# Ten closing steps split by token half: five weight blocks kept instead of reloaded, more entry products, and weight casts two blocks ahead

## The chip, the cores and the metric

The program runs on one core of a Trainium2 chip. The metric is the device time of one execution in microseconds. Five engines work side by side, each through its own queue of instructions in order: TensorE (PE, matmuls; PEld are its weight loads), VectorE (DVE), ScalarE (ACT), GpSimd (POOL) and SyncE (SP, which here issues all DMAs). They wait for each other by semaphores.

## The reference, cut to what matters

One decoder layer over 256 tokens of width 2048 in float32. A vector `mod`, made from the condition `c`, gives nine groups of shift, scale and gate; each is 2048 wide.

```python
cond = silu(c)
mod = cond @ ada_w + ada_b                  # 9 x 2048: sh1 sc1 gt1 sh2 sc2 gt2 sh3 sc3 gt3
h = rmsnorm(x, norm_g[0]) * (1 + sc1) + sh1
x = x + 0.5 * gt1 * ((silu(h @ wg) * (h @ wu)) @ wd)      # FFN 1, d_ff 5632
h = rmsnorm(x, norm_g[1]) * (1 + sc2) + sh2
x = x + gt2 * mixer(h)                      # 8 forgetting-attention heads, 8 gated-delta heads, w_in, w_out
h = rmsnorm(x, norm_g[2]) * (1 + sc3) + sh3
x = x + 0.5 * gt3 * ((silu(h @ wg) * (h @ wu)) @ wd)      # FFN 2
return rmsnorm(x, final_norm)
```

Each stage needs the normalised x of the stage before, so a token's last sum, its squares, its root and its scaling stand between two stages.

## The kernel before, in words

**Weights.** All large weights come as a stream of blocks: 128 x 1024 float32 (512 KB, eight tiles of 128 x 128), in the order in which they are used. `Stream.block` (L98) issues a block's DMA on SP into a tile `wraw` and casts it on ACT to `whi` (L106, a shorter float format). `Stream.low` (L109) subtracts on DVE: `wlo` = raw - `whi` (L113). Activations are split in the same way into a high and a low part (`hs`, `hid`, `oh`). There are three places each for `wraw`, `whi` and `wlo`, and in the FFNs and at the mixer's end a fourth (`W.more`), taken by each block whose number leaves 3 when divided by 4. `Stream.next` (L126) hands out the next tiles; at each new block it also adds a pace (`RATE`, by block number) to a sum, and whenever this reaches 1 it fetches one more column of the condition's matrix (`ada_col`; DMA `adat`, 1 MB, and a reduction on DVE, L286, three blocks later), unless `W.quiet` is set. With `W.early` (the mixer's projections) a block's load, cast and subtraction are written in the program one block ahead of its use (`ahead`).

**Products.** `products` (L572) multiplies a step (four tiles, 512 output columns) by the two halves of the tokens: for each half three matmuls, high x high (L576), low x high (L577), high x low (L579). In the mixer's projections by rows the three are L857, L858, L859; by columns, L517 and L518.

**Stages.** `ffn` runs `gate_up` and `down` for two parts of d_ff each; `mixer` runs projections, the heads' chains (a planner with due times puts pieces of them between the projections' tiles) and the output product `po`. A stage's last 512 output columns are made in `last_block` (L665). Its last ten steps (`S_OUT`) are first done for half 0 alone, then for half 1 alone, so that half 0's sum, squares, root and scaling can run while PE works on half 1. The weights of the last four of these steps are held in the usual places; those of the first six (`S_AGAIN`, `twice`) are fetched a second time as three further blocks, cast and subtracted again, for half 1. There are three such ends: FFN 1, mixer, FFN 2. Then one block of the next stage is loaded ahead, its cast tied behind half 0's root (`roots[0]`), its subtraction behind half 0's factor (`yins[0]`).

**Entries.** `modulate` (L425) first makes sure that all columns of the next stage's shift and scale are there (`ada_need`), builds the gains, and makes a list of work: `half(0)` and `half(1)` (rows of `hs` 0 and 1 for one token half: scale x to `xn`, transpose on PE into `pxt`, then ACT and DVE write the high and low parts, L448 to L453), then pairs of rows for both halves. It is called two steps before the end, with `half(0)`. The next stage does its first `S_IN` = 2 row groups for half 0 alone (four products in the mixer, six in FFN 2), then the same for half 1, then the rest for both. `residual` (L534) is the sum at a stage's end: gate multiply (`rs`, L540), add (L541), square (L384), and in the last columns `norm_rstd` (L396 to L401).

The framework orders each engine's queue by a simulated schedule in which program order sets the priority; `tc.issue_after` ties an instruction behind another of the same engine.

Of the kernel before, what the change touches and what calls it, by code (L numbers as in the profile page):

```python
# [16 lines left out]
P = 128  # L17
# [12 lines left out]
S_OUT, S_AGAIN, S_IN = 10, 6, 2  # L30
# [7 lines left out]
N_TILES = 5392 + 3 * 4 * S_AGAIN  # L38
# [4 lines left out]
RATE = ((0, 0.5), (24, 0.34), (56, 0.45), (68, 0.35), (112, 0.45), (168, 0.38), (266, 0.4), (282, 0.0), (300, 0.17), (412, 0.125))  # L43
# [33 lines left out]
class Stream:  # L77


    def __init__(self, nc, w, raw, hi, lo):  # L80
# [9 lines left out]
        self.pairs, self.early, self.ready = set(), set(), {}  # L90
# [6 lines left out]

    def block(self, b, cast_after=None):  # L98

        at = PAIR if b in self.pairs else 0  # L100
        raw, hi, lo = self.more if self.more and b % 4 == 3 else (self.raw, self.hi, self.lo)
        r = raw.tile([P, WB * P], F32, name="wraw")
        self.last = self.nc.sync.dma_start(r, self.w[b]).ins
        self.h = hi.tile([P, WB * P + 64], F32R, name="whi")[:, at : at + WB * P]
        with nullcontext() if cast_after is None else self.tc.issue_after(cast_after):
            self.cast = self.nc.scalar.copy(self.h, r).ins  # L106
        return r, lo, at

    def low(self, r, lo, at):  # L109

        self.l = lo.tile([P, WB * P + 64], F32R, name="wlo")[:, at : at + WB * P]
# [14 lines left out]
    def next(self, mat, k, n, width=1):  # L126
        i = len(self.order)
        if i % WB == 0:
# [8 lines left out]
            if b + 1 in self.early:  # L137
                self.ahead(b + 1)
# [13 lines left out]
def layer_kernel(ctx: ExitStack, tc: tile.TileContext, xrow, c, adaw, cols, cst, fng, w, out, order, dbg=None):  # L152
# [272 lines left out]
    def modulate(which, m_sh, m_sc):  # L425
# [3 lines left out]

        def turn(ps, j, t):  # L430

            xn = tmp.tile([P, T], F32, name="xn", bufs=4)
            if t:
                V.tensor_scalar(xn, X(t, j * P, T), ystd[t], None, ALU.mult)
            else:
                A.activation(xn, X(t, j * P, T), AF.Copy, scale=ystd[t])
# [18 lines left out]
        def half(t):  # L455

            ps = psf("pxt")
            turn(ps, 0, t)
            for j in range(2):
                scale(ps, j, t * P, P)  # L460
# [14 lines left out]
    hq = {"todo": []}  # L475

    def h_need(k, t=1):

        while hq["todo"] and (hq["todo"][0][0] < k + AHEAD if hq["todo"][0][0] > 1 and t else hq["todo"][0][:2] <= (1, t)):
            hq["todo"].pop(0)[2]()  # L480
# [106 lines left out]
    def gate_up(which, f0, f1, hp, sp, chunks, lead, need):  # L587
# [55 lines left out]
        for ci, (k0, k1) in enumerate(chunks):  # L643
            for gi in range(0, len(cgs), 2):
# [6 lines left out]
                first = S_IN if need is h_need and pb else 0  # L651
                wts = {(k, e): one(pb[e], *e, k, k0, k1, (0,)) for k in range(k0, k0 + first) for e in pb}
                for (k, e), wt in wts.items():
                    one(pb[e], *e, k, k0, k1, (1,), wt)
                for k in range(k0 + first, ks):
                    for e in pb:
                        one(pb[e], *e, k, k0, k1)
# [7 lines left out]
    def last_block(steps, weights, one, ps, m_gt, squares, begin):  # L665

        twice, held = steps[-S_OUT : S_AGAIN - S_OUT], steps[S_AGAIN - S_OUT :]
        for f in steps[:-S_OUT]:
            one(f, weights(f), (0, 1), False)
        for f in twice:  # L670
            one(f, weights(f), (0,), False)
        held = [(f, weights(f)) for f in held]
        for f, wt in held:
            one(f, wt, (0,), f == steps[-1])
# [5 lines left out]
        for i in range(1, n):  # L680
            W.ahead(b + i)
        for f, wt in held:
            one(f, wt, (1,), False)
        if squares != "final":
            W.held = [yins[0]]
            W.ahead(b + n, roots[0])
        for f in twice:
            if f == twice[-2] and begin:
                modulate(*begin)
                hq["todo"].pop(0)[2]()  # L690
# [792 lines left out]
```

## Time and profile before

| what | us |
|---|---|
| median of 3 runs | 2037.12 |
| lowest, highest | 2032.08, 2038.51 |
| profiled execution | 2035.86 |
| its span, first to last instruction | 2034.1 |
| mean granted TensorE clock | 0.991 |

In the views, a busy row gives start or span, the engine, the source line, the operation and the tiles out<-in; square brackets hold the idle time of the engine just before and what ended it. A windows row gives the length of the window, the busy time of PE, PEld, DVE, ACT and POOL (with the number of instructions), the granted TensorE clock, the share of time in which DMA engines were busy, and GB/s.

### The profile page before, as it was taken

The numbers are of one execution on the slowest core, as the hardware profiler recorded it, in microseconds if no ns is written. First come the engines' busy times: TensorE is split into PE (matmuls) and PEld (weight loads), VectorE is DVE, ScalarE is ACT, GpSimd is POOL, SyncE is SP. The second block draws the span as 40 slices with busy tenths as digits, with TensorE's granted clock in tenths as the row PEclk, the third lists the DMA queues.
The fourth block names the chain that finished last, engine by engine and source line by source line (L and its number), as shares of the span: only waits on it lengthen the run. The fifth ranks groups of instructions, "written<-read, shape, count | busy, mean of one in ns | idle before, by whom it ended". The sixth has DMA issues, their size and how long they took to land.

```text
span 2034.1 us, 25528 instructions
## 1 busy us (share of the span) xinstructions
PE 1987.4 (98%) x9385; PEld 1648.0 (81%) x9385; DVE 1494.7 (73%) x2096; ACT 1001.4 (49%) x1451; POOL 2.6 (0%) x15
## 2 busy tenths in 40 slices
PE   8999999999999999998999999999999999999998
PEld 5788888888888887887888888788888888888886
DVE  6899999898787886689877887765566565455455
ACT  5544444343433456685657655644444333444444
POOL 0000000000000000000000000000000000000000
PEclk8999999999999999999999999999999999999999
DMA  8989898999788886564656577666666665555554
GB/s 323 349 326 349 314 344 333 354 387 375 298 331 338 325 304 243 185 214 155 209 205 220 187 259 267 219 218 239 249 243 231 239 238 196 187 192 189 207 195 167
DMA packets 134511, 528.92 MB, mean 260 GB/s; under 512 B 18489, under 2 KB 23785, under 8 KB 116081
## 3 DMA queue, kind: packets, MB, share of 16 engines
q1 hardware_dynamic: 134386, 527.29, 71.2%
q8 instruction: 73, 1.20, 0.2%
q14 instruction: 52, 0.43, 0.1%
HBM read 521.82 MB, written 5.41 MB: 259 GB/s over the span
## 4 chain that ended last, share of the span: by engine, by line
PE 91%; DVE 3%; DMA 3%; ACT 2%; issue 1%; ACTq 0%; DVEq 0%; SPq 0%
PE pgu L579 15%; PE pgu L577 15%; PE pgu L576 15%; PE pd L577 8%; PE pd L576 8%; PE pd L579 8%; PE pp L517 6%; PE pp L518 3%; DMA wraw<-in_w_dram 2%; DVE wlo L113 2%; PE pv L857 1%; PE pv L859 1%; PE pv L858 1%; PE po L577 1%; PE po L576 1%; PE po L579 1%
## 5 line engine op out<-in xcount | busy, mean ns | idle before, releaser
L106 ACT CAST whi<-wraw 128x1024 fp32r<-128x1024 f32 x683 | 714.8, 1051 | 833.7 <-PE pgu L577 280.3
L113 DVE TENSOR_TENSOR wlo<-wraw,whi 128x1024 fp32r<-128x1024 f32 x683 | 826.3, 1222 | 385.9 <-ACT whi L106 382.8
L576 PE MATMUL pgu<-whi,hs 128*128 128x512 f32 x1408 | 552.1, 394 | 14.8 <-ACT hs L411 6.5
L577 PE MATMUL pgu<-whi,hs 128*128 128x512 f32 x1408 | 550.5, 392 | 0.3
L579 PE MATMUL pgu<-wlo,hs 128*128 128x512 f32 x1408 | 438.0, 391 | 1.2 <-DVE wlo L113 1.2
L286 DVE CUSTOM_DVE_ANT_0 adat<-adat,cs,colt 128x2048 f32<-128x2048 f32 x140 | 328.7, 2348 | 41.4 <-DMA adat<-in_ada_dram 40.6
L576 PEld LDWEIGHTS pgu<-whi,hs 128*128 128x128 f32 x1408 | 266.0, 189 | 73.4 <-ACT hs L411 7.4
L579 PEld LDWEIGHTS pgu<-wlo,hs 128*128 128x128 f32 x1408 | 265.1, 189 | 58.4 <-DVE wlo L113 3.2
L577 PEld LDWEIGHTS pgu<-whi,hs 128*128 128x128 f32 x1408 | 266.2, 189 | 56.6 <-DVE hs L453 1.1
L576 PE MATMUL pd<-whi,hid 128*128 128x512 f32 x704 | 274.7, 390 | 0.0
L577 PE MATMUL pd<-whi,hid 128*128 128x512 f32 x704 | 273.9, 389 | 0.0
L517 PE MATMUL pp<-hs,whi 128*128 128x512 f32 x656 | 242.3, 405 | 8.7 <-ACT whi L106 8.7
L579 PE MATMUL pd<-wlo,hid 128*128 128x512 f32 x704 | 220.0, 389 | 0.0
L518 PE MATMUL pp<-hs,wlo 128*128 128x256 f32 x656 | 189.7, 290 | 1.3 <-DVE wlo L113 1.3
L576 PEld LDWEIGHTS pd<-whi,hid 128*128 128x128 f32 x704 | 132.2, 188 | 27.7 <-issue 0.2
L579 PEld LDWEIGHTS pd<-wlo,hid 128*128 128x128 f32 x704 | 132.2, 188 | 27.5
L577 PEld LDWEIGHTS pd<-whi,hid 128*128 128x128 f32 x704 | 132.2, 188 | 27.1
L517 PEld LDWEIGHTS pp<-hs,whi 128*128 128x128 f32 x656 | 124.8, 190 | 32.1 <-ACT whi L106 9.9
L518 PEld LDWEIGHTS pp<-hs,wlo 128*128 128x128 f32 x656 | 125.5, 191 | 2.5 <-DVE wlo L113 1.9
L857 PE MATMUL pv<-whi,hs 128*128 128x512 f32 x128 | 52.3, 411 | 0.5 <-ACT whi L106 0.3
L859 PE MATMUL pv<-wlo,hs 128*128 128x512 f32 x128 | 50.8, 398 | 0.0
L858 PE MATMUL pv<-whi,hs 128*128 128x512 f32 x128 | 50.6, 395 | 0.0
(313 smaller groups left out, 1369.9 us busy)
## 6 DMA issues: line engine op xcount, KB each, us to landing
wraw<-in_w_dram SPq DMA_DIRECT2D x683, 512.0 KB, 4.4
adat<-in_ada_dram SPq DMA_DIRECT2D x140, 1024.0 KB, 7.6
gtr<-gd SPq DMA_DIRECT2D x12, 256.0 KB, 6.2
rw<-rowd SPq DMA_DIRECT2D x24, 128.0 KB, 3.8
adaf<-in_ada_dram SPq DMA_DIRECT2D x4, 512.0 KB, 10.0
x<-in_xr_dram SPq DMA_DIRECT2D x4, 512.0 KB
adaf<-in_ada_dram SPq DMA_DIRECT2D x2, 1024.0 KB
xd<-x SPq DMA_DIRECT2D x4, 512.0 KB
```

Of the source, the lines that this page charges most:

```text
L106: self.cast = self.nc.scalar.copy(self.h, r).ins
L113: self.sub = self.nc.vector.tensor_tensor(self.l, r, self.h.bitcast(F32), ALU.subtract).ins
L286: V.tensor_tensor_reduce(t, t, cs, HALF.get(m, 1.0), L("adab", q, 1), ALU.mult, ALU.add, mod[:, q : q + 1])
L517: PE.matmul(ps, wt[0], act.rearrange("p a t -> p (a t)"), start=first, stop=False)
L518: PE.matmul(ps[:, :T], wt[1], act[:, 0], start=False, stop=last)
L576: PE.matmul(ps[t], hi_(t), wh, start=first, stop=False)
L577: PE.matmul(ps[t], lo_(t), wh, start=False, stop=False)
L579: PE.matmul(ps[t], hi_(t), wl, start=False, stop=last)
L857: PE.matmul(pv[m][t], hs[:, k, 0, sl], wh, start=(k == 0), stop=False)
L858: PE.matmul(pv[m][t], hs[:, k, 1, sl], wh, start=False, stop=False)
L859: PE.matmul(pv[m][t], hs[:, k, 0, sl], wl, start=False, stop=(k == KD - 1))
```

## The change

What it does:

- The last ten steps' five blocks are all kept until half 1. The first three go, high and low part together, into one tile each of a pool that has room inside the stage (`home`: the FFN's `hid` pool; in the mixer a new pool `holdp` of three, opened after the heads' pools are closed). The last two stay in the usual places. Half 1 takes these two first, then the three. No block is loaded a second time: the stream has 5392 tiles (674 blocks) instead of 5464 (683).
- While half 1 runs, three blocks of the next stage are loaded, cast and subtracted: one before half 0's sum, one after two steps, its cast behind `roots[0]`, one after four.
- `modulate` makes the work list finer (`n_ahead` = 2: rows 0 to 3 in pieces of one half); two pieces of half 0 are done at the end. Half 1's first `xn` is written directly behind its root, and the next block's subtraction is tied behind it.
- At entries eight products of half 0 (FFN 2) or six (mixer) come before half 1's, four blocks or three.
- In the mixer's projections a block's load is written three blocks ahead and its cast and subtraction two ahead. The pace of adaLN columns is 0.25 from block 338 on (0.17 before), and it is silenced from the middle of the mixer's third output block on.

The diff, cut to its core:

```diff
-S_OUT, S_AGAIN, S_IN = 10, 6, 2
+S_OUT, S_HOME = 10, 6
-RATE = ((0, 0.5), (24, 0.34), (56, 0.45), (68, 0.35), (112, 0.45), (168, 0.38), (266, 0.4), (282, 0.0), (300, 0.17), (412, 0.125))
+RATE = ((0, 0.5), (24, 0.34), (56, 0.45), (68, 0.35), (112, 0.45), (168, 0.38), (266, 0.4), (282, 0.0), (300, 0.17), (338, 0.25), (412, 0.125))
...
+    def load(self, b):
+
+        more = self.more and self.home is None and b % 4 == self.odd
+        r = (self.more[0] if more else self.raw).tile([P, WB * P], F32, name="wraw")
+        self.last = self.nc.sync.dma_start(r, self.w[b]).ins
+        return r, more
...
+        r, more = self.loaded.pop(b) if b in self.loaded else self.load(b)
+        hi, lo = self.more[1:] if more else (self.hi, self.lo)
+        if self.home:
+            both = self.home()
+            self.h, lo = both[:, : WB * P], both[:, WB * P :]
+        else:
+            self.h = hi.tile([P, WB * P + 64], F32R, name="whi")[:, at : at + WB * P]
+        if cast_after is None and self.cast_held:
+            cast_after = self.cast_held.pop(0)
...
-            if b + 1 in self.early:
-                self.ahead(b + 1)
+            if b + 3 in self.early:
+                self.loaded[b + 3] = self.load(b + 3)
+            for a in (b + 1, b + 2):
+                if a in self.early and a not in self.ready:
+                    self.ahead(a)
...
-        hq["todo"] = [(1, 0, lambda: half(0)), (1, 1, lambda: half(1))]
-        hq["todo"] += [(j + 1, 1, lambda j=j: pair(j)) for j in range(2, KD, 2)]
+        js = range(0, 2 * n_ahead, 2)
+        hq["todo"] = [((j, t), lambda j=j, t=t: half(j, t)) for t in range(2) for j in js]
+        hq["todo"] += [((j, None), lambda j=j: pair(j)) for j in range(2 * n_ahead, KD, 2)]
+        hq["normed"] = normed
...
-                first = S_IN if need is h_need and pb else 0
+                ahead = [(k, e) for k in range(k0, ks) for e in pb]
+                n = 8 if hq["todo"] else 0
...
+        W.home = home
+        held = []
+        for f in steps[-S_OUT:]:
+            if len(held) == S_HOME:
+                W.home = None
+            held.append((f, weights(f)))
+            one(f, held[-1][1], (0,), f == steps[-1])
+        held = held[S_HOME:] + held[:S_HOME]
         assert len(W.order) % WB == 0 and not W.ready
         b = len(W.order) // WB
-        n = S_AGAIN * 4 // WB
-        W.ahead(b)
+        if begin:
+            W.more, W.odd = None, (b + 3) % 4
+            W.ahead(b)
         residual(ps[0], 0, 3, m_gt, squares)
+        W.held = [yins[0]]
+        for n, (f, wt) in enumerate(held):
+            if begin and n == 2:
+                W.ahead(b + 1, roots[0])
+            if begin and n == 4:
+                W.ahead(b + 2)
+            if begin and n == S_OUT - 2:
+                modulate(*begin)
+                for _ in range(begin[-1]):
+                    h_pop()
+            one(f, wt, (1,), n == S_OUT - 1)
         residual(ps[1], 1, 3, m_gt, squares, yins[0])
+        if begin:
+            W.held = [sums[1], hq["normed"](0, 1)]
+            W.cast_held = [None, roots[1]]
...
+            n = 6 if hq["todo"] else 0
             held = []
+            for m, k in todo[:n]:
+                held.append((m, k, W.next(m, k, 4 * grp, 4)))
+                some(m, k, (0,), held[-1][2])
+            for i, (m, k, wt) in enumerate(held):
                 some(m, k, (1,), wt)
+                if i == 1:
+                    W.ahead(len(W.order) // WB)
+            if n:
+                W.early = set(range(len(W.order) // WB + 1, W.last_early))
...
+                if (b, i) == (2, KD // 2):
+                    W.quiet = True
...
+                holdp = mx.enter_context(tc.tile_pool(name="holdp", bufs=S_HOME // 2))
```

More of the change, by code (lines that the diff above doesn't have):

```diff
@@ L89, in __init__ @@
         self.sub = None
-        self.pairs, self.early, self.ready = set(), set(), {}
+        self.pairs, self.early, self.ready, self.loaded = set(), set(), {}, {}
+        self.home, self.odd, self.cast_held = None, 3, []
     def behind(self, later=True):
@@ L428, in modulate, with normed @@
         W.quiet = True
-        def turn(ps, j, t):
[L432 to L436, printed above, removed]
+        made = {}
+        def normed(j, t):
+            xn = made[j, t] = tmp.tile([P, T], F32, name="xn", bufs=4)
+            if t:
+                return V.tensor_scalar(xn, X(t, j * P, T), ystd[t], None, ALU.mult).ins
+            return A.activation(xn, X(t, j * P, T), AF.Copy, scale=ystd[t]).ins
+        def turn(ps, j, t):
+            if (j, t) not in made:
+                normed(j, t)
+            xn = made.pop((j, t))
             for q in range(2):
@@ L453, in scale, with half @@
             V.tensor_tensor(hs[:, j, 1, tok], t, hs[:, j, 0, tok].bitcast(F32), ALU.subtract)
-        def half(t):
+        def half(j, t):
             ps = psf("pxt")
-            turn(ps, 0, t)
-            for j in range(2):
-                scale(ps, j, t * P, P)
+            turn(ps, j, t)
+            for q in range(2):
+                scale(ps, j + q, t * P, P)
         def pair(j):
@@ L663, in gate_up, with last_block, down @@
         return hid
-    def last_block(steps, weights, one, ps, m_gt, squares, begin):
-        twice, held = steps[-S_OUT : S_AGAIN - S_OUT], steps[S_AGAIN - S_OUT :]
+    def last_block(steps, weights, one, ps, m_gt, squares, begin, home):
         for f in steps[:-S_OUT]:
             one(f, weights(f), (0, 1), False)
[L670 to L674, printed above, removed]
+        W.home = home
[6 more added lines that the diff above has]
+        held = held[S_HOME:] + held[:S_HOME]
         assert len(W.order) % WB == 0 and not W.ready
         b = len(W.order) // WB
-        n = S_AGAIN * 4 // WB
-        W.ahead(b)
+        if begin:
+            W.more, W.odd = None, (b + 3) % 4
+            W.ahead(b)
         residual(ps[0], 0, 3, m_gt, squares)
[L680 to L688, printed above, removed]
+        W.held = [yins[0]]
[5 more added lines that the diff above has]
+            if begin and n == S_OUT - 2:
                 modulate(*begin)
-                hq["todo"].pop(0)[2]()
-            one(f, weights(f), (1,), f == twice[-1])
+                for _ in range(begin[-1]):
+                    h_pop()
+            one(f, wt, (1,), n == S_OUT - 1)
         residual(ps[1], 1, 3, m_gt, squares, yins[0])
-        if squares != "final":
-            W.held = [sums[1], yins[1]]
-    def down(which, f0, f1, hid, m_gt, squares, begin=None):
+        if begin:
+            W.held = [sums[1], hq["normed"](0, 1)]
+            W.cast_held = [None, roots[1]]
+    def down(which, f0, f1, hid, m_gt, squares, hp, begin=None):
         fs = list(range(f0, f1))
@@ L705, in down @@
             if ends:
-                last_block(fs, lambda f: W.next(("d", which), f, 4 * b, 4), one, ps, m_gt, squares, begin)
+                home = lambda: hp.tile([P, 2 * WB * P], F32R, name="hold", tag="hid")
+                last_block(fs, lambda f: W.next(("d", which), f, 4 * b, 4), one, ps, m_gt, squares, begin, home)
             else:
@@ L732, in ffn @@
                     fng_load()
-                down(which, f_[half], f_[half + 1], hid, m_gt, *((squares, begin) if half else (None,)))
+                down(which, f_[half], f_[half + 1], hid, m_gt, *((squares, hp, begin) if half else (None, hp)))
             W.more = None
@@ L1329, in mixer @@
             if b == 3:
-                last_block(list(range(KD)), weights, one, ps, 5, "mid", (2, 6, 7))
+                last_block(list(range(KD)), weights, one, ps, 5, "mid", (2, 6, 7, 2),
+                           lambda: holdp.tile([P, 2 * WB * P], F32R, name="hold"))
                 break
```

42 lines of the change are left out of this document (18 added, 24 removed).

## The prediction

> **What bounds the kernel now.** I read the page's head first, then the grouped waits of the matmul engine, then the windows view in 20 us slices, and only then the timelines of the slices that are not full.
>
> ```profile
> PE 1987.4 (98%) x9385; PEld 1648.0 (81%) x9385; DVE 1494.7 (73%) x2096; ACT 1001.4 (49%) x1451; POOL 2.6 (0%) x15
> L106 ACT CAST whi<-wraw 128x1024 fp32r<-128x1024 f32 x683 | 714.8, 1051 | 833.7 <-PE pgu L577 280.3
> L113 DVE TENSOR_TENSOR wlo<-wraw,whi 128x1024 fp32r<-128x1024 f32 x683 | 826.3, 1222 | 385.9 <-ACT whi L106 382.8
> PE pp L517 <- ACT whi L106: 8.7, 4, 2.9
> 759.17 0.39 PE L576 MATMUL pd<-whi,hid 128*128 128x512 f32 x1
> 759.40 0.39 PE L577 MATMUL pd<-whi,hid 128*128 128x512 f32 x1
> 759.62 0.39 PE L579 MATMUL pd<-wlo,hid 128*128 128x512 f32 x1
> ```
>
> PE is busy 98%: matmuls start every 0.227 us, and the change neither adds nor removes one. So it can win only where PE stands still or runs at a lower clock. A product of one token half is three matmuls, 0.68 us; a block of weights is two steps, 1.36 us for one half and 2.72 us for both.
>
> The places, by the windows view (length, then PE, PEld, DVE, ACT, POOL busy, granted clock, DMA share, GB/s):
>
> ```profile
> 774.00:778.00 4.00, 1.62 (x7) 0.69 (x6) 2.94 (x9) 2.79 (x6) 0.00 (x0) 1.00 0.92 330
> 778.00:784.00 6.00, 5.86 (x21) 4.23 (x22) 3.76 (x10) 3.29 (x10) 1.30 (x5) 0.72 0.92 325
> 880.00:900.00 20.00, 16.74 (x94) 14.39 (x93) 17.95 (x63) 19.09 (x56) 0.12 (x1) 0.91 0.73 221
> 920.00:940.00 20.00, 18.02 (x107) 16.09 (x108) 17.87 (x47) 9.91 (x22) 0.55 (x3) 0.91 0.64 202
> 880.00:960.00 80.00, 70.95 (x425) 61.98 (x423) 73.53 (x248) 58.56 (x144) 0.66 (x4) 0.96 0.57 185
> 1060.00:1220.00 160.00, 157.13 (x941) 135.74 (x940) 129.97 (x320) 102.47 (x221) 0.00 (x0) 1.00 0.63 220
> 1284.00:1288.00 4.00, 0.22 (x1) 0.00 (x0) 4.00 (x6) 1.98 (x3) 0.00 (x0) 0.99 0.41 133
> 1288.00:1296.00 8.00, 7.66 (x21) 5.59 (x22) 5.45 (x13) 2.41 (x8) 0.00 (x0) 0.58 0.49 166
> ```
>
> First entry (first FFN to mixer, 772 us): 4 - 1.62 = 2.38 us idle, 0.14 more, and 6 x 0.28 = 1.68 us at the lower clock: 4.2 us. Second entry (mixer to second FFN, 1284 us): 3.78 + 0.34 idle and 8 x 0.42 = 3.36 us of clock: 7.5 us. The mixer at 880 to 960 us: 80 - 70.95 = 9.05 us idle and, in two slices, 2 x 20 x 0.09 = 3.6 us of clock. The first 130 us and the chain behind PE's last product are touched by no edit.
>
> **Part 1, the last ten steps.** Nine blocks (three at each of three ends) are no longer loaded twice: nine casts of 1.05 us, nine subtractions of 1.22 us, nine transfers of 512 KB. All lie beside a full PE, so they are worth nothing by themselves; what they leave is room. In the mixer's end a reload's cast stood at the head of ACT, waiting for PE to free a place, with half 0's square behind it:
>
> ```profile
> 1278.33 1.05 ACT L106 CAST whi<-wraw 128x1024 fp32r<-128x1024 f32 x1 [3.02 <-PE po L577]
> 1279.29 0.62 ACT L384 ACTIVATE jq<-x 128x512 bf16<-128x512 f32 x1
> 763.39 3.54 SPq L826 DMA_DIRECT2D xd<-x  x3
> ```
>
> With five blocks kept (three in inner places that need no release, two in the usual three), the third usual place takes the next stage's first block, and the second and third follow as half 1 frees places: all three are cast and subtracted before the stage begins, where before only one was. Also, at 763.39 three copies of x sat 3.5 us at the head of SP's queue until half 0's x was there; they are tied behind the last weight load issued, which is now the third block's, so these loads no longer wait behind them.
>
> **Part 2, more products at entries.** Half 1's chain (gate, sum, square, root, normalise, transpose, scale) sets when its products can start. At the first entry:
>
> ```profile
> 771.86 0.69 DVE L540 TENSOR_TENSOR rs<-pd,gtr 128x512 f32<-128x512 f32 x1 [0.16 <-PE pd L579]
> 773.39 0.62 ACT L384 ACTIVATE jq<-x 128x512 bf16<-128x512 f32 x1
> 774.53 1.05 ACT L106 CAST whi<-wraw 128x1024 fp32r<-128x1024 f32 x1 [0.41 <-DMA wraw<-in_w_dram]
> 775.48 0.29 ACT L396 ACTIVATE nstd<-ss 128x1 f32<-128x1 f32 x1
> 776.26 0.16 DVE L401 SCALAR_TENSOR_TENSOR nstd<-nya,nstd 128x1 f32<-128x1 f32 x1
> 777.47 0.61 DVE L434 TENSOR_SCALAR xn<-x,nstd 128x256 f32<-128x256 f32 x2
> 777.87 0.88 PE L439 MATMUL pxt<-colt,xn 128*128 128x128 f32 x6 [2.33 <-DVE xn L434]
> 778.35 0.46 ACT L451 ACTIVATE hs<-pxt,mod,g 128x128 fp32r<-128x128 f32 x1 [0.32 <-PE pxt L439]
> ```
>
> The reader sees a cast of 1.05 us (late because its transfer was late) between square and root, and 1.2 us between the factor (776.42) and xn (777.47) in which DVE subtracted a block. Without these two, and with x right behind rs, the chain is rs 0.69, x 0.69, square and its read 0.75, root 0.3, four small DVE operations 0.6 to 0.7, xn 0.35: 3.4 us from the end of half 1. The change issues xn first by name and has the three blocks ready. Half 0 then has six products (4.1 us) instead of four (2.7 us) to cover it. What stays open is transposes, scale and their hand-over if they stand behind the six products: from 777.87 to the end of 778.35 + 0.46 is 0.94 us. I take 1.1 us left of 4.2: **3.1 us** gained; bounds 0.5 (the chain as late as now, only two products more) and 4.2.
>
> At the second entry two adaLN reductions stand in DVE before half 1's chain:
>
> ```profile
> 1283.82 0.40 PE L579 MATMUL po<-wlo,oh 128*128 128x512 f32 x1
> 1281.15 2.35 DVE L286 CUSTOM_DVE_ANT_0 adat<-adat,cs,colt 128x2048 f32<-128x2048 f32 x1
> 1284.56 2.35 DVE L286 CUSTOM_DVE_ANT_0 adat<-adat,cs,colt 128x2048 f32<-128x2048 f32 x1
> 1286.83 0.69 DVE L540 TENSOR_TENSOR rs<-po,gtr 128x512 f32<-128x512 f32 x1
> 1287.43 0.17 DVE L422 SCALAR_TENSOR_TENSOR g<-mod,colt 128x16 f32<-128x16 f32 x1
> 1287.69 0.46 ACT L451 ACTIVATE hs<-pxt,mod,g 128x128 fp32r<-128x128 f32 x1 [1.82 <-DVE g L422]
> L275 SPq DMA_DIRECT2D adat<-in_ada_dram x21: 328/425/1977, 809.9 to 1274.3; - x21
> ```
>
> PE's last product ended at 1284.2, rs came 2.6 us later, and even half 0's rows waited for the gains. In the new pace the mixer must fetch the same 21 columns. Counted by blocks, now three lower: five blocks at 0.40 (2.0), 38 at 0.17 (6.5), then 0.25 from block 338; the remaining 12.5 take 50 blocks, to 388, and the pace is silenced at 398. So both reductions leave the entry. The 5.5 us of eight half-0 products then cover a chain of 3.4 us plus scaling. Two things are late next: the hand-over again (0.9), and the fourth block, which eight products need after six (4.1 us). Its place opens only when the old tiles over it are free, in my estimate at half 1's last product. The windows show such a transfer: issued at 1284.7, gone by 1287.5.
>
> ```profile
> L103 SPq DMA_DIRECT2D wraw<-in_w_dram x4: 327/328/328, 1284.7 to 1293.5; - x4
> 1285.50:1287.50 2.00, 0.00 (x0) 0.00 (x0) 2.00 (x4) 0.38 (x1) 0.00 (x0) 1.00 0.81 262
> ```
>
> 2.8 us and a cast of 1.05 make 3.9 to 4.1 us: just in time, or some tenths late. I take 1.3 us left of 7.5: **6.2 us** gained; bounds 3.0 and 7.5.
>
> The waits that are added: the fourth block's subtraction behind half 1's sum, the fifth's cast behind its root and its subtraction behind xn. PE needs none of them before about 4 us after half 1, and the chain goes ahead of them. Two more transposes in the end phase are moved, not added.
>
> **Part 3, mixer blocks cast two ahead, loaded three ahead.** The waits on casts, in the order of time:
>
> ```profile
> 940.00:960.00 20.00, 17.04 (x113) 14.83 (x111) 19.07 (x72) 14.55 (x38) 0.00 (x0) 1.00 0.24 86
> 893.86 0.50 PE L517 MATMUL pp<-hs,whi 128*128 128x512 f32 x1 [2.57 <-ACT whi L106]
> 921.98 0.50 PE L517 MATMUL pp<-hs,whi 128*128 128x512 f32 x1 [2.82 <-ACT whi L106]
> 958.22 0.51 PE L517 MATMUL pp<-hs,whi 128*128 128x512 f32 x1 [2.88 <-ACT whi L106]
> ACT whi L106 <- PE pp L517: 25.9, 18, 3.8
> ```
>
> Each time the cast stood in ACT behind the heads' chains. One block earlier in the program is 2.7 us and more of stock for PE, about the length of each wait. The first two would go: 2.57 + 2.82 and the clock of 3.6, 9.0 us. But DVE is busy 73.53 of 80 us there: it has 6.5 us to spare, and work that is put off comes back as a wait for a chain (as behind 958.22, where DVE was full). I take the 6.5 as the cap. The higher pace puts 38 x 0.08 = 3 columns more, 7 us, on DVE between about 1055 and 1200 us, where it has 30 us free in 160; I take 0.5 for it (bounds 0 and 7). Sum **6.0 us**; bounds -3 (the order of every queue there changes) and 16 (all idle and all clock from 880 us on). A load three ahead waits in SP for its place, with row loads, adaLN columns and the heads' solves behind it; the place is free by then, as its block was subtracted two blocks before: nothing.
>
> **Sum.** 3.1 + 6.2 + 6.0 = 15.3 us. The profiled execution took 2035.9 us (span 2034.1); the median shown is 2037.1, 1.2 above. 2035.9 - 15.3 = **2020.6 us**.
>
> **The rivals.**
> - *DVE is the mixer's bound* and its waits only move: entries alone, 2035.9 - 9.3 = 2026.6. For it: DVE at 92% there; against: three waits name ACT's cast. Chance 0.20.
> - *The entries stay starved*, because the transposes are queued where half 1's chain isn't ready: only the two reductions go, of which some 3 us count: 2035.9 - 3.0 - 6.0 = 2026.9. Chance 0.10. If mixer and entries both fail, or the kept blocks wait for their places so that the change doesn't do what it says, 2033; 0.08.
> - *The lower clock does not come back with the shorter stalls*, so that its 1.68 and 3.6 us stay: the first entry wins 3.1 - 1.7 = 1.4, the mixer 2.57 + 2.82 - 0.5 = 4.9, and the time is 2035.9 - 1.4 - 6.2 - 4.9 = 2023.4. For it: the window from 940 to 960 us holds a wait of 2.88 us, and its slice has a full clock. Against: 2.4 us of idleness at the first entry were followed by 0.72. Chance 0.05. [...]
> - *Slower: a cast at the head of ACT's queue.* Cast two ahead, each needs the place of the block that PE is just finishing. ACT then stands, and with it the heads' copies and exponentials that PE's own chain matmuls need. Today 18 such waits are 25.9 us, 1.44 each, mostly harmless. If as many more reach PE: 2035.9 - 9.3 + 25.9 = 2052.5. It decides from (9.3 + 6.1) / 1.44 = 11 such waits. For it: three places stay three; against: PE reaches the block that frees the place before it reaches the chains that follow. Chance 0.07. [...]
>
> **How the numbers follow.** Forecast 0.50 (2013 to 2026), rivals as given. The range takes in the first two rivals and the clock's, and leaves out most of the slower one and of the double failure: 2012.5 to 2031.5. About 0.3%, 6.1 us, is what a measurement of this kernel can tell from no change: faster than that 0.81, within 0.12 (the double failure and the upper edge of the two starved cases), slower 0.07.
>
> **What would show it.** Right: 674 casts; no adaLN reduction between the mixer's half-1 sums and the next stage; at the entries a PE gap under 1.5 us and a clock above 0.9 behind it; PE's waits on L106 in the mixer under 4 us. Wrong: transposes waiting on xn for over 2 us, a first product waiting for the fourth block's cast, or new PE waits on heads' tiles (qv, on, orw) that add up to more than the casts' waits do now. The sum falls if the schedule moves the mixer by more than the entries win.

## The result, and the profile after

The changed kernel takes 2024.15 us (median of 4 runs, 2023.22 to 2024.68) against 2035.73 us for the kernel before, timed alongside (4 runs, 2032.08 to 2038.51): ratio 0.994, 95% interval 0.9923 to 0.9958. The profiled execution took 2023.22 us, its span is 2021.4 us (before 2034.1), the mean granted clock 0.993 (before 0.991). The forecast was 2020.6 with a range of 2012.5 to 2031.5. So sign and range hold. The sum doesn't: the two entries won more than their terms, and the mixer's term was not won.

I cut both profiled executions at the same events on PE: first matmul of the mixer (`pv`), first `pp`, first output product (`po` from `whi` and `oh`), first `pgu` of FFN 2, first and last `pd` of it.

| stretch | before, us | after, us | difference |
|---|---|---|---|
| start to first `pv` (FFN 1) | 771.7 | 769.4 | -2.3 |
| first `pv` to first `pp` (entry 1) | 52.8 | 48.2 | -4.6 |
| first `pp` to first `po` (heads) | 363.4 | 365.3 | +1.9 |
| first `po` to first `pgu` (output product, wait of entry 2) | 100.3 | 95.0 | -5.3 |
| first `pgu` to first `pd` (its lower clock too) | 274.0 | 271.7 | -2.3 |
| first `pd` to last | 462.5 | 462.3 | -0.2 |
| rest | 9.4 | 9.5 | +0.1 |

The sum is -12.7, the difference of the spans. The first row belongs to no edit: it arises in the first 130 us, where both kernels have the same instructions in the same order, and other kernels of this study, with the same start, show 768.4 to 772.9. Without it the changed stretches won some 10 us.

The page after (its head and two rows of its costliest groups):

```profile
PE 1985.9 (98%) x9385; PEld 1645.1 (81%) x9385; DVE 1483.2 (73%) x2093; ACT 993.7 (49%) x1448; POOL 2.6 (0%) x15
L126 DVE TENSOR_TENSOR wlo<-wraw,whi 128x1024 fp32r<-128x1024 f32 x665 | 804.5, 1221 | 399.8 <-ACT whi L119 396.4
L119 ACT CAST whi<-wraw 128x1024 fp32r<-128x1024 f32 x665 | 696.9, 1053 | 807.4 <-PE pgu L610 291.7
```

665 blocks go to the usual places and 9 to the kept ones, 674 in all: the change does what it says.

The entries, by the windows view (16 us each, columns as before):

```profile
768.00:784.00 16.00, 15.58 (x73) 12.06 (x73) 11.36 (x30) 11.76 (x25) 1.31 (x5) 1.00 0.64 208
1276.00:1292.00 16.00, 14.88 (x71) 11.67 (x69) 11.91 (x28) 11.79 (x25) 0.00 (x0) 1.00 0.51 161
```

PE stands still for 0.42 us at the first and 1.12 us at the second, and the clock stays at 1.00 in both. Before, 4.2 and 7.5 us were lost there. The timeline of the first entry, DVE and PE, shows half 1's chain with nothing foreign in it but three small subtractions of `hs`:

```profile
769.58 0.69 DVE L573 TENSOR_TENSOR rs<-pd,gtr 128x512 f32<-128x512 f32 x1
770.19 0.69 DVE L476 TENSOR_TENSOR hs<-ht,hs 128x128 fp32r<-128x128 f32 x3
770.79 0.68 DVE L574 TENSOR_TENSOR x<-x,rs 128x512 f32<-128x512 f32 x1
773.24 0.88 DVE L452 TENSOR_SCALAR xn<-x,nstd 128x256 f32<-128x256 f32 x3
...
773.24 0.39 PE L896 MATMUL pv<-wlo,hs 128*128 128x512 f32 x1
773.65 0.77 PE L462 MATMUL pxt<-colt,xn 128*128 128x128 f32 x4
774.64 0.73 PE L894 MATMUL pv<-whi,hs 128*128 128x512 f32 x2 [0.22 <-ACT hs L474]
775.54 0.50 PE L895 MATMUL pv<-whi,hs 128*128 128x512 f32 x1 [0.17 <-DVE hs L476]
```

Half 0's six products end at about 773.6, `xn` begins at 773.24, and the transposes follow without a wait. At the second entry `rs` starts at 1278.11, as PE's last product of half 1 ends (1277.68 + 0.39), where before it came 2.6 us late; no adaLN reduction stands between. Of the eight half-0 products in the program PE ran six (18 matmuls) ahead of half 1's transposes, as many as before. What remains is the fourth block's cast, the last wait on PE below; the cast itself follows PE's transposes:

```profile
1277.68 0.39 PE L612 MATMUL po<-hold,oh 128*128 128x512 f32 x1
1278.11 0.69 DVE L573 TENSOR_TENSOR rs<-po,gtr 128x512 f32<-128x512 f32 x1
1282.94 1.04 ACT L119 CAST whi<-wraw 128x1024 fp32r<-128x1024 f32 x1 [1.45 <-PE pxt L462]
1284.04 0.50 PE L609 MATMUL pgu<-whi,hs 128*128 128x512 f32 x1 [1.09 <-ACT whi L119]
```

The heads' dense stretch is another matter. The grouped waits of PE between 830 and 1200 us, and the windows of the stretch:

```profile
PE pp L550 <- ACT whi L119: 4.2, 4, 2.5
PE pp L551 <- DVE wlo L126: 3.2, 3, 1.9
PE pk L1041 <- ACT kk L1048: 0.9, 1, 0.9
...
860.00:1000.00 140.00, 132.52 (x812) 115.71 (x811) 123.92 (x382) 99.51 (x232) 0.67 (x4) 0.96 0.59 192
```

The waits on the cast fell from 8.7 us to 4.2, but those on the subtraction grew from 1.3 to 3.2; the waits on the heads' own tiles stay near 2 us. The windows from first `pp` to first `po`, the kernel before and then the changed kernel:

```profile
824.50:1187.90 363.40, 350.88 (x2114) 306.77 (x2113) 299.41 (x791) 244.14 (x534) 0.66 (x4) 0.99 0.58 197
817.60:1182.90 365.30, 355.33 (x2114) 307.26 (x2112) 303.81 (x794) 244.47 (x534) 0.67 (x4) 0.99 0.60 205
```

PE's idle time fell by 2.5 us (12.5 to 10.0), but PE is busy 4.4 us longer with the same 2114 matmuls. About 1.7 us of that is a lower clock (from 860 to 1000 us it is 0.96, before 0.98); the rest wasn't located. DVE has 4.4 us more work in the stretch. So there is no gain. The +1.9 us itself is no shown loss: `a_act`, `a_dve`, `a_few` and `a_n1` below, which leave the heads as in the changed kernel, show 363.1 to 367.4 us.

### The profile page after: what moved, and what is told of

It is laid out like the page before. It is cut to its first block, busy times and chain, and to the rows that moved or that the text cites. A ratio compares the mean times of both kernels' runs of the same rounds, so it can differ in the third digit from the quotient of the medians.

```text
span 2021.4 us, 25472 instructions
## 1 busy us (share of the span) xinstructions
PE 1985.9 (98%) x9385; PEld 1645.1 (81%) x9385; DVE 1483.2 (73%) x2093; ACT 993.7 (49%) x1448; POOL 2.6 (0%) x15
## 4 chain that ended last, share of the span: by engine, by line
PE 91%; DVE 4%; ACT 2%; issue 1%; DMA 1%; SPq 0%; ACTq 0%; DVEq 0%
PE pgu L612 15%; PE pgu L609 15%; PE pgu L610 15%; PE pd L612 8%; PE pd L610 8%; PE pd L609 8%; PE pp L550 6%; PE pp L551 3%; PE pv L895 1%; PE pv L896 1%; PE pv L894 1%; DVE wlo L126 1%; PE po L610 1%; PE po L612 1%; PE po L609 1%
## 5 line engine op out<-in xcount | busy, mean ns | idle before, releaser
L126 DVE TENSOR_TENSOR wlo<-wraw,whi 128x1024 fp32r<-128x1024 f32 x665 | 804.5, 1221 | 399.8 <-ACT whi L119 396.4
L119 ACT CAST whi<-wraw 128x1024 fp32r<-128x1024 f32 x665 | 696.9, 1053 | 807.4 <-PE pgu L610 291.7
L609 PE MATMUL pd<-whi,hid 128*128 128x512 f32 x680 | 265.2, 390 | 0.0
L610 PE MATMUL pd<-whi,hid 128*128 128x512 f32 x680 | 264.6, 389 | 0.0
L550 PE MATMUL pp<-hs,whi 128*128 128x512 f32 x656 | 241.6, 403 | 4.2 <-ACT whi L119 4.2
L612 PE MATMUL pd<-wlo,hid 128*128 128x512 f32 x680 | 210.8, 389 | 0.0
L551 PE MATMUL pp<-hs,wlo 128*128 128x256 f32 x656 | 191.7, 293 | 3.2 <-DVE wlo L126 3.2
L612 PEld LDWEIGHTS pd<-wlo,hid 128*128 128x128 f32 x680 | 127.5, 188 | 27.1 <-DVE wlo L126 0.8
L609 PEld LDWEIGHTS pd<-whi,hid 128*128 128x128 f32 x680 | 127.7, 188 | 26.7
L610 PEld LDWEIGHTS pd<-whi,hid 128*128 128x128 f32 x680 | 127.7, 188 | 26.4
L550 PEld LDWEIGHTS pp<-hs,whi 128*128 128x128 f32 x656 | 125.1, 191 | 27.5 <-ACT whi L119 5.2
L551 PEld LDWEIGHTS pp<-hs,wlo 128*128 128x128 f32 x656 | 125.7, 192 | 5.0 <-DVE wlo L126 4.1
```

Of the source, the lines that this page charges most:

```text
L126: self.sub = self.nc.vector.tensor_tensor(self.l, r, self.h.bitcast(F32), ALU.subtract).ins
L550: PE.matmul(ps, wt[0], act.rearrange("p a t -> p (a t)"), start=first, stop=False)
L551: PE.matmul(ps[:, :T], wt[1], act[:, 0], start=False, stop=last)
L609: PE.matmul(ps[t], hi_(t), wh, start=first, stop=False)
L610: PE.matmul(ps[t], lo_(t), wh, start=False, stop=False)
L612: PE.matmul(ps[t], hi_(t), wl, start=False, stop=last)
```

## The experiments

The question was where the mixer's 6.0 us stayed and what won the entries. Times are medians; ratios are to runs of the kernel before taken alongside.

**Casts two ahead: undone on the changed kernel (`a_one`), done alone on the kernel before (`b_two`).**

```diff
# a_one, on the changed kernel
-            if b + 3 in self.early:
+            far = b < 284
+            if far and b + 3 in self.early:
...
-            for a in (b + 1, b + 2):
+            for a in (b + 1, b + 2) if far else (b + 1,):
```

> The changed kernel, but in the heads' part of the mixer (from block 284 on) a block's load, cast and subtraction are written one block ahead again; entries and pace stay. Prediction's theory (two ahead is worth 6 us, because the waits of PE on ACT's casts go): the heads' stretch from the first to the last projection by columns, 365.3 us after the change, becomes 369 to 372 us, the time about 2030 us, with three waits of over 2 us on casts back. Rival, VectorE bounds this stretch and waits only move: 363 to 367 us, the time 2022 to 2027 us. Third theory, two ahead itself costs some 2 us there (it was 363.4 us before the change): about 2022 us.

2019.43 us (2017.63 to 2022.29, 6 runs), ratio 0.9924 (0.9912 to 0.9937). Against the changed kernel this is 4.7 us less by the medians and 3.3 by the ratios, whose intervals overlap a little. All six runs lie below the twelve of the changed kernel and of `a_dve` and `a_act` below (2022.49 us and up), though not all were timed alongside. The heads take 360.7 us, 4.6 less than in the changed kernel, which with the time is below all three expectations; the entries are the same (48.2; first `po` to first `pgu` 94.9).

```diff
# b_two, on the kernel before
-            if b + 1 in self.early:
-                self.ahead(b + 1)
+            far = b >= 287
+            for a in (b + 1, b + 2, b + 3):
+                if far and a in self.early and a not in self.ready and a not in self.loaded:
+                    self.loaded[a] = self.load(a)
+            for a in (b + 1, b + 2) if far else (b + 1,):
+                if a in self.early and a not in self.ready:
+                    self.ahead(a)
```

> The kernel before, with only one edit: from block 287 on (heads' part of the mixer) loads are written three blocks ahead, casts and subtractions two. Prediction's theory: the heads' stretch falls from 363.4 us by about 6 us, the time to about 2030 us, and PE's waits on casts there from 8.7 us to under 4 us. Rival, VectorE bounds it: 362 to 367 us, the time 2034 to 2038 us; cast waits may fall, but waits on subtractions and on heads' tiles take their place.

2030.14 us (11 runs), ratio 0.9974 (0.9964 to 0.9983). Heads 360.7, which is 2.7 less than before (the profiled run, 2027.11, is the fastest of the eleven). PE's waits on weights from 815 to 1195 us:

```profile
PE pp L529 <- DVE wlo L119: 3.0, 3, 1.9
...
PE pp L528 <- ACT whi L112: 0.5, 1, 0.5
```

Here the time and the waits on casts (0.5 us, before 8.7) are those of the prediction's theory; the heads won less than half of its 6 us, and the waits on subtractions grew from 1.3 to 3.0. So one edit wins on one kernel and costs on the other: it reorders the queues, and what comes of that depends on all the rest. The stall between 880 and 900 us shows it. First row the changed kernel, two ahead:

```profile
886.52 0.38 PE L551 MATMUL pp<-hs,wlo 128*128 128x256 f32 x1 [1.94 <-DVE wlo L126]
```

and `a_one`, one ahead:

```profile
890.48 0.51 PE L551 MATMUL pp<-hs,whi 128*128 128x512 f32 x1 [2.57 <-ACT whi L119]
893.03 0.58 PE L552 MATMUL pp<-hs,wlo 128*128 128x256 f32 x1 [1.10 <-DVE wlo L126]
```

The slices from 880 to 900 us hold 3.3 to 4.1 us of idle PE in both kernels and in `b_two`; two ahead moves the name in the bracket from the cast to the subtraction.

**Is it DVE or ACT? Extra work on each (`a_dve`, `a_act`, then `a_dve2`, `a_act2`).** The first pair copied a constant:

```diff
# a_dve (a_act: A.copy)
+            if 298 <= b < 320:
+                self.extra()
...
+        j3 = tmp.tile([P, 512], F32, name="rs")
+        V.tensor_copy(j3, cs[:, :512])
```

> The changed kernel with 22 more copies of 128x512 on VectorE, one at each block from 298 to 319 (the heads' stretch between some 880 and 965 us); nothing reads them. If VectorE bounds this stretch, PE's idle time and lost clock between 860 and 1000 us (7.5 and 5.2 us in the changed kernel) grow by most of the copies' sum (22 times 0.4 to 0.6 us, 9 to 13 us) and the time by 5 to 12 us, to 2029 to 2036 us. If ScalarE's queue with its casts and table loads bounds it, by under 3 us.

> The changed kernel with the same 22 copies on ScalarE instead (0.6 us each, 14 us together). If VectorE bounds the stretch: under 3 us more. If ScalarE does: 5 to 12 us more.

`a_dve` 2025.52 (4 runs, 0.9956, 0.994 to 0.9971), `a_act` 2024.02 (4 runs, 0.9948, 0.9934 to 0.9963). Both miss the question: the copies waited for nothing late, and the schedule put them at 771 to 802 us, into the first entry (49.1 and 48.8 us in place of 48.2); none ran between 860 and 1000 us. For the heads they stand as near repeats of the changed kernel: 364.0 and 363.1. The second pair reads the weight block in use, so that it can't leave:

```diff
# a_dve2 (a_act2: A.copy)
-        V.tensor_copy(j3, cs[:, :512])
+        V.tensor_copy(j3, W.h.bitcast(F32)[:, :512])
```

> The changed kernel with 22 more copies of 128x512 on DVE, one at each weight block from 298 to 319 (about 860 to 930 us); each reads the whi of the current block, so that it can't leave the stretch, and nothing reads what it writes. Their price is taken from the run, an estimate of 0.35 to 0.7 us each by the tensor operations of that size: 8 to 15 us of work. Theory A, DVE bounds the heads' dense stretch (it had 123.9 of 140 us busy there, so 16 us free): heads (first pp to first po) grow from 365.3 to 371 us or more, 2030 us or more in all. Theory B, the order in the queues and ACT's casts bound it, DVE's free time takes the copies up: heads within 3 us, 2024 to 2027.

> The same 22 copies on ACT in place of DVE, an estimate of 0.5 to 0.6 us each: 11 to 13 us of work. ACT had 99.5 of 140 us busy there. Theory A (DVE is the bound): the copies lie in ACT's free 40 us, heads within 3 us of 365.3, 2022 to 2027. Theory B (casts stand behind other work in ACT's queue, PE's waits name them): heads 370 us or more, 2029 us or more, and PE's waits on L119 in the heads grow from 6.5 us to over 10.

The copies by their source line, first `a_dve2`, then `a_act2` (ns least/median/most, first and last start):

```profile
L379 DVE COPY rs<-whi x22: 407/412/428, 873.5 to 972.9; 128x512 f32<-128x512 f32 x22
```

```profile
L379 ACT COPY rs<-whi x22: 602/611/627, 882.7 to 954.3; 128x512 f32<-128x512 f32 x22
```

On DVE 22 x 0.412 = 9.1 us of work made the heads 371.8 us, 6.5 more than in the changed kernel, and the time 2029.6 (9 runs, 0.9971, 0.9961 to 0.9981). On ACT 22 x 0.611 = 13.4 us left them at 365.5 (+0.2), and the time at 2022.44 (4 runs, 0.9942, 0.9927 to 0.9957). The waits and the window of `a_dve2`:

```profile
957.27 0.58 PE L560 MATMUL pp<-hs,wlo 128*128 128x256 f32 x1 [5.59 <-DVE wlo L126]
...
860.00:1000.00 140.00, 127.95 (x778) 111.73 (x777) 127.97 (x402) 101.44 (x236) 0.67 (x4) 0.95 0.56 183
```

In the changed kernel DVE had 16 us free of 140, and yet 9.1 us of added work lengthened the heads by 0.7 us for each us. By the medians it cost 5.5 us against the changed kernel and 7.2 against `a_act2` (the profiled run of `a_dve2` is the slowest of its nine). Its free time isn't where the chains are due: from 934 us until the subtraction of that 5.59 us wait ended at 957.2, DVE's timeline names no idle time (from 940 to 960 us it is busy 19.86 of 20). ACT's 40 free us took 13.4 for nothing. So DVE bounds the stretch in the changed kernel, although the waits of before named ACT's cast. One side effect is small: a copy keeps its `whi` place until it has run, and one cast waited 1.8 us for that in `a_dve2`.

**The pace (`b_rate`, `a_late`, `a_oldpace`).** `b_rate` puts the new pace alone on the kernel before:

```diff
-(300, 0.17), (412, 0.125))
+(300, 0.17), (341, 0.25), (412, 0.125))
...
+                if (b, i) == (2, KD // 2):
+                    W.quiet = True
```

> The kernel before, with only the pace of adaLN columns changed: 0.25 from block 341 on, silenced from the middle of the mixer's third output block. The two reductions leave the second entry. Prediction: some 3 us of the 7.5 us lost at that entry come back (the sum of half 1 starts 2.6 us earlier, and half 0's rows no longer wait for the gains), the rest needs the kept blocks and the products: 2031 to 2034 us. Rival: half 1's chain was late anyway, by the casts and reloaded blocks: under 1 us, about 2036 us. A third: a shorter stall also spares the lower clock, so that 5 us or more come back: 2030 us.

2032.29 us (11 runs), ratio 0.9988 (0.998 to 0.9997), in the first expectation's range. First `po` to first `pd` is 4.4 us shorter, the heads are 3.8 longer (367.2). The second entry of this kernel:

```profile
1284.00:1300.00 16.00, 15.06 (x68) 11.34 (x67) 12.93 (x29) 12.24 (x25) 0.00 (x0) 1.00 0.47 154
```

PE is idle for 0.94 us at a full clock, where the kernel before lost 7.5 us. So the pace alone, without kept blocks or ready blocks, clears this entry by about as much as the whole change does (1.12 us idle): more than the 3 us expected here. The stretch from first `po` shows only 4.4 us of it, because a stall near 1212 us, which the kernel before has too, is followed by a lower clock in this execution (from 1200 to 1220 us 1.77 us idle and a clock of 0.91; the kernel before has 1.50 us and 1.00). `a_oldpace` takes the pace out of the changed kernel:

```diff
-(300, 0.17), (338, 0.25), (412, 0.125))
+(300, 0.17), (412, 0.125))
...
-                if (b, i) == (2, KD // 2):
-                    W.quiet = True
```

> The changed kernel with the old pace of the adaLN columns: no step to 0.25 at block 338, no quiet from the middle of the third output block on. Theory: what the pace wins at the second entry, it gives back in the heads, as it did when it was put on the kernel before (entry 2 -4.4, heads +3.8). So reductions are back between the mixer's half-1 sums and the second FFN, the stretch from the first po to the first pd +3 to +5 us (366.7 now), heads -2 to -4 (365.3 now), in all 2022 to 2027. Rival, my step as predicted (the pace costs 0.5 in the heads and the two reductions cost the entry over 2 us): 2027 to 2030.

2026.17 us (4 runs), ratio 0.9953 (0.9938 to 0.9967). First `po` to first `pd` 371.6 in place of 366.7, +4.9; heads 363.5, -1.8. This is the first expectation, though -1.8 is within the heads' spread: the pace wins 2.0 us by the medians and about 3 by these stretches; the intervals overlap. At the entry one reduction of 2.35 us is back, now behind half 0's chain, and the transposes wait:

```profile
1276.17 2.35 DVE L302 CUSTOM_DVE_ANT_0 adat<-adat,cs,colt 128x2048 f32<-128x2048 f32 x1
...
1277.96 1.09 PE L462 MATMUL pxt<-colt,xn 128*128 128x128 f32 x4 [2.39 <-ACT xn L453]
1283.51 0.51 PE L610 MATMUL pgu<-whi,hs 128*128 128x512 f32 x1 [0.95 <-DVE hs L476]
```

`a_late` keeps the dense stretch free of columns: 0.17 from block 300 is gone, 26 blocks or 4.4 columns of 2.35 us, 10.4 us of DVE, moved behind it.

```diff
-(300, 0.17), (338, 0.25), (412, 0.125))
+(326, 0.265), (412, 0.125))
```

> The changed kernel with another pace of adaLN columns: none from block 282 to 325, then 0.265 (instead of 0.17 from 300 and 0.25 from 338). No fewer columns in all, but the three or four reductions of 2.35 us that lie between 860 and 960 us now come after about 1000 us. If VectorE bounds the heads' first chains: 7 to 9 us less work for it there, PE's idle time and lost clock in 880 to 960 us (7.3 and 5.2 us) fall by half or more, and the time falls by 4 to 9 us, to 2015 to 2020 us. If the order of ACT's queue decides: no clear change, 2022 to 2027 us.

2020.53 us (5 runs), ratio 0.9933 (0.992 to 0.9946); heads 361.9, -3.4. The dense stretch:

```profile
860.00:1000.00 140.00, 134.47 (x834) 116.36 (x833) 119.46 (x378) 102.83 (x244) 0.66 (x4) 0.99 0.53 165
```

Less work on DVE there (one reduction in place of five), and PE's idle time falls from 7.5 to 5.5 us and the clock rises to 0.99. This points the same way as `a_dve2`, but doesn't show it by itself: the time lies between the two expectations, and the interval overlaps the changed kernel's. The columns come back later: from 1000 to 1190 us PE is idle 4.1 us against 2.5.

**What won the entries (`a_few`, `a_n1`).** `a_few` goes back to four and six products of half 0:

```diff
-                n = 8 if hq["todo"] else 0
+                n = 6 if hq["todo"] else 0
...
-            n = 6 if hq["todo"] else 0
+            n = 4 if hq["todo"] else 0
```

> The changed kernel with the old number of half-0 products at the entries: four in the mixer, six in FFN 2 (three blocks, so that nothing waits for the fourth). In the changed kernel half 1's xn is there 4.0 us after the end of half 1 and the transposes stand right behind six products (4.1 us). Theory: with four products (2.7 us) the first entry's PE gap grows by 1.3 to 1.5 us, to about 1.9 us; at the second the 1.09 us wait for the fourth block's cast goes and half 1's scaling takes its place, so nothing is won. Time +1 to +2 us against the changed kernel, 2025 to 2026 us. Rival: the extra products matter for the clock too (a gap of 2 us is followed by half rate): +3 us or more, over 2027 us. Other rival: they were not needed: no change.

Entry 1 takes 48.2 us as before the edit, and the wait for the fourth block at entry 2 is 0.8 us. But this run doesn't test the products, because the schedule put the same number in front again. The matmuls into `pv` from their first one to half 1's transposes, in the kernel before, the changed kernel and `a_few` (length, then PE, PEld and ACT busy, and the last three columns as above):

```profile
771.50:777.80 6.30, 3.48 (x12) 1.98 (x12) 0.00 (x0) 1.00 0.93 349
769.20:773.60 4.40, 4.22 (x18) 3.33 (x18) 0.00 (x0) 1.00 0.97 379
769.00:773.40 4.40, 4.20 (x18) 3.35 (x18) 0.00 (x0) 1.00 0.89 330
```

With four products in the program PE still ran 18 matmuls, six products, before the transposes: the half-0 parts of the next two steps went ahead of half 1, which wasn't ready. At entry 2, too, 18 stand there in both. The time, 2026.38 (5 runs, 0.9956, 0.9944 to 0.9969), is 2.2 higher, with overlapping intervals, and in the profile the difference lies in the heads (367.4), where the edit does nothing but shift the queues. `a_n1` readies one block only and ties the later ones as the kernel before did:

```diff
-            if begin and n == 2:
-                W.ahead(b + 1, roots[0])
-            if begin and n == 4:
-                W.ahead(b + 2)
...
-            W.held = [sums[1], hq["normed"](0, 1)]
-            W.cast_held = [None, roots[1]]
+            hq["normed"](0, 1)
+            W.held = [sums[1], yins[1]]
```

> The changed kernel, where only one block of the next stage is loaded, cast and subtracted before half 1's last product; the second and third come when the stage asks for them, and the holds on the fourth and fifth are those of the kernel before (sums and root of half 1 on the next two subtractions). Six and eight half-0 products stay. Theory A, ready blocks win the entries: at the first entry products wait for the second block's cast, 2 to 3 us more there (48.2 now), and 2 to 3 at the second: 2027 to 2031. Theory B, the kept blocks and the chain without a cast or a subtraction in it win them, and loads come early enough without a word: within 1.5 us of now, 2022.5 to 2026.

2025.22 us (4 runs), ratio 0.9955 (0.9938 to 0.9972), as theory B has it. Entry 1 takes 49.5, +1.3 (the kernels with this entry as in the changed one, but for the two with copies in it, show 48.2); first `po` to first `pd` 366.5, unchanged. The waits of PE at the first entry:

```profile
PE pv L892 <- DVE wlo L126: 0.9, 1, 0.9
PE pv L890 <- ACT hs L474: 0.3, 1, 0.3
PE pv L891 <- DVE hs L476: 0.2, 1, 0.2
```

The ACT and DVE timelines of `a_n1` show why this costs so little: the second and third block were loaded and cast before half 1 ended without being asked for, since nothing is loaded twice and places and queues were free. Only their subtractions came late, behind x and behind the root:

```profile
766.19 1.04 ACT L119 CAST whi<-wraw 128x1024 fp32r<-128x1024 f32 x1
767.94 1.03 ACT L119 CAST whi<-wraw 128x1024 fp32r<-128x1024 f32 x1
...
772.36 1.22 DVE L126 TENSOR_TENSOR wlo<-wraw,whi 128x1024 fp32r<-128x1024 f32 x1
774.09 1.22 DVE L126 TENSOR_TENSOR wlo<-wraw,whi 128x1024 fp32r<-128x1024 f32 x1
```

Before, a cast stood at 774.53 in half 1's chain, late by its own transfer. So the explicit readying of two blocks carries 1.3 of the first entry's 4.6 us. What both kernels keep is that the last blocks aren't loaded again, so that casts leave the chain, and that six products stand in front of half 1 and half 0's second piece is done before the entry. No run separates these three.

**Both mixer findings together (`c_best`).** One ahead from block 284 on, and columns out of the dense stretch:

```diff
# a_one's edit, and
-(266, 0.4), (282, 0.0), (300, 0.17), (338, 0.25), (412, 0.125))
+(266, 0.45), (288, 0.0), (326, 0.225), (412, 0.125))
```

> The changed kernel with casts one block ahead in the heads' part (as in a_one) and the columns moved out of the dense stretch: pace 0.45 for blocks 266 to 287 (the projections by rows, where VectorE is busy 9 to 15 of 20 us), none from 288 to 325, 0.225 after. If VectorE's load decides, this adds a_late's gain to a_one's: heads' stretch 357 to 360 us, time 2015 to 2018 us. If a_one's and a_late's gains are one and the same (a queue order that happens to fit), 2018 to 2022 us.

2019.29 us (2017.66 to 2021.45, 5 runs), ratio 0.9921 (0.9908 to 0.9933), heads 362.6. It is no better than `a_one`, as the second expectation has it: the two gains don't add. Both beat the kernel before, and both have shorter heads than the changed kernel; all runs of `c_best` lie below all of `a_few`, `a_dve` and `a_act`, timed alongside.

## Why the prediction was right in sign and wrong in its sum

- *What bounds the kernel.* Right: PE is busy 98% in both, and what was won is idle time and clock at the two entries.
- *Entry 1, 3.1 predicted, 4.6 measured.* Mechanism right, term too small. I kept 1.1 us for transposes, scaling and their hand-over; 0.42 us stayed, and the clock's 1.68 us came back whole. The chain from half 1's end to `xn` took 4.0 us instead of my 3.4 (three `hs` subtractions slipped between `rs` and x), and the six products covered it. The window accounts for 3.8 of the 4.6; the rest I put down to the second piece of half 0's transposes, which now run ahead of the first `pv`. This is argued, not shown. Of the causes, only the ready second and third block are priced, at 1.3 (`a_n1`). The trace speaks for the extra products: four would have ended after 2.7 us, and the chain took 4.0; but no run took them away. One reading was off: between factor and `xn` lay 777.47 - 776.42 = 1.05 us, not 1.2.
- *Entry 2, 6.2 predicted, about 6.4 measured in the window* (7.6 with the output product, of which about 1 us lies near 1200 us). The size is right, also what is late next: the fourth block's cast, 1.09 us, of the 1.3 that I left. The cause is narrower than I had it. The pace alone left 0.94 of the 7.5 us on the kernel before (`b_rate`), and eight products never stood ahead of half 1's transposes. The pace has a price in the heads, 1.8 us by `a_oldpace` and 3.8 alone on the kernel before (single profiles, whose spread is as large), where the step had 0.5. I had taken that from DVE's free time between 1060 and 1220 us as a mean.
- *Mixer, 6.0 predicted, nothing won (+1.9 us in this pair of profiles).* This step failed: "One block earlier in the program is 2.7 us and more of stock for PE, about the length of each wait." Alone on the kernel before, it did take the waits on casts away (8.7 to 0.5 us), but the heads won 2.7 us in place of the term's 6.5, and waits on subtractions grew; in the changed kernel the waits on casts stayed at 4.2 us, just above the 4 that I had set as the sign of being right, and nothing was won. A place in the program is only a priority for the schedule, not a place in a queue (the copies of `a_dve` and the products of `a_few` moved), and the stock has to be made by DVE, which had none to give where it was due. I read 73.53 of 80 us as 6.5 us to spare; `a_dve2` shows that added DVE work comes back at 0.7 of its length while 16 of 140 us look free. The first rival, DVE is the mixer's bound and its waits only move (2026.6, chance 0.20), had the mechanism; its time is 3.4 us above the profiled 2023.22, because the entries won 2.9 us more and the first FFN ran 2.3 us faster, less the heads' 1.9.
- *The total* came within 4 us of the forecast by luck: the mixer's term was 7.9 us too high, and against it the entries won 2.9 us more than I gave them and 2.3 us of run-to-run difference went the same way.
- *The other rivals.* The entries did not stay starved. The clock came back at both entries, but in the heads it fell (0.96 in place of 0.98 from 860 to 1000 us). No cast at the head of ACT's queue stopped the heads: PE's waits on ACT's tiles of the heads are 0.9 us, and `a_act2` shows ACT with room.
- *Still open*: why two ahead wins 2.7 us in the heads of the kernel before and loses 4.6 in those of the changed one. DVE as the bound says that order decides there, not which instruction of the order does. Idle time and lost clock from 840 to 1200 us differ by only 2.2 us between the changed kernel and `a_one`; the remaining 2.4 lies in time that counts as PE busy and wasn't located. Also open is how the first entry's gain divides between the kept blocks, the two products and half 0's second piece.

## What to carry to other kernels

When a wait names the cast, look at what the engine behind it in the chain (here DVE with the subtraction) still has free at that place, and test it by adding work that is tied to the place by its input; a mean of free time over 80 us proves nothing. A stage entry is won by clearing the chain between the last sum and the first operand: two reductions out of DVE's way were worth some 6.5 us at the second one. Where a schedule orders the queues, count in the trace what really stands in front before you credit or blame an edit of program order. Measure an edit of order on the kernel in which it will stand: the same one gained 4.6 us on one kernel and cost 3 to 5 on the other.

## What the runs showed of the hardware

Stalls of the same kind are followed by a lower clock in some executions and not in others. From 940 to 960 us the kernel before had a wait of 2.88 us and a full clock; the changed kernel had 3.53 us idle in two waits and a clock of 0.83, and `a_act2` 1.50 us idle and a clock of 1.00:

```profile
940.00:960.00 20.00, 16.47 (x89) 14.23 (x88) 17.11 (x60) 11.81 (x28) 0.00 (x0) 0.83 0.43 130
```

```profile
940.00:960.00 20.00, 18.50 (x117) 16.17 (x116) 19.27 (x64) 15.94 (x37) 0.00 (x0) 1.00 0.63 198
```

The clock records of two traces, those of the kernel before and of the changed kernel, show what differs. In both, the granted clock is 1.00 or 0.50, and from its first change on it switches only at multiples of 3.41 us. What goes with a fall there is the idle time within one such stretch, not the length of a wait. Four stretches of the kernel before, the first two at the first entry, the other two across the wait of 2.88 us that ended at 958.22:

```profile
775.94:779.35 3.41, 1.37 (x8) 0.93 (x8) 3.34 (x8) 2.46 (x5) 0.00 (x0) 1.00 0.89 309
779.35:782.77 3.42, 3.39 (x9) 2.48 (x8) 2.41 (x8) 2.22 (x6) 0.07 (x1) 0.50 0.99 321
953.44:956.85 3.41, 1.81 (x11) 1.09 (x9) 3.38 (x14) 1.79 (x3) 0.00 (x0) 1.00 0.12 44
956.85:960.27 3.42, 1.82 (x13) 1.55 (x13) 3.19 (x14) 2.47 (x8) 0.00 (x0) 1.00 0.08 18
```

The wait of 2.33 us put 2.04 us of idleness into one stretch, and the next ran at half rate. The longer one was cut in two by a boundary, 1.60 us on each side, and cost no clock. The changed kernel's wait of 2.53 us, which ended at 947.80, put 2.10 us into one stretch, and the next two ran at half rate. In these two traces every full-rate stretch with 1.94 us or more of idle PE was followed by one at half rate, and none with 1.84 us or less. By the granted clock a stretch at half rate costs half of its 3.41 us, 1.7 us. The matmuls say nearly as much: in the changed kernel a pair of L550 and L551 takes 0.64 us at the clock of 0.50 (953.80 to 954.44) and 0.35 us at 1.00 (941.51 to 941.86), an estimate of 3.41 x (1 - 0.35 / 0.64) = 1.5 us. So where a stall falls decided over that much here. Near repeats of one kernel (the changed kernel, `a_dve`, `a_act`) differ by one such stretch between 860 and 1000 us (a clock of 0.96, 0.98 and 0.98), so a difference of 2 us in one profile of the heads is not yet an effect of an edit.
